# Row maxima from the high parts alone, with query tiles paired on the lower and the upper rows of the array

## The chip, the cores and the metric

The kernel runs on one core of a Trainium2 chip. Its time is in microseconds (us) of the device, and the number that counts is the median of several runs. A core has TensorE (PE in the profile; its weight loads are listed apart, as PEld), VectorE (DVE), ScalarE (ACT), GpSimd (POOL) and SyncE (SP, which here only issues DMAs). PE reads its two operands from SBUF and writes to PSUM banks; DVE and ACT read PSUM. Each engine works through its instructions in the order in which the program lists them.

## The reference, cut to what matters

One encoder layer is applied to 2048 + 256 tokens with a model width of 1024: a norm, one input projection, a bidirectional mLSTM on eight heads beside grouped-query attention on eight heads, an output projection, and a gated feed-forward block with a convolution. The attention is the part that counts here:

```
q = rmsnorm(aq per head); k = rmsnorm(ak per head); both rotated
s = q @ k^T / 8                     # per head, 64 wide, fp32
p = softmax(s, axis=-1)             # minus the row's maximum, exp, divided by the sum
o = p @ v                           # 4 query heads share one key/value head
```

The maximum that a softmax takes away leaves the result as it is, whatever number is taken away, as long as the exponentials neither overflow nor vanish.

## The kernel before, in words

Every fp32 operand of a large matmul is split into a high part in the type fp32r and the rest, its low part, and a product is the sum of high x high, high x low and low x high.

The program has five stages. Stage A projects q, k, v and the gates. Then two Python generators are run against each other by `run_both`: `attention` and `mlstm`. It counts the costs that each yields (constants such as `A_PAIR`, `A_MAX`, `A_PREP` for attention) and picks whichever is behind; a scheduler with priorities then orders the instructions on each engine, so that matmuls of the two stand mixed. When `mlstm` has ended, `attention` goes on beside `phase_c`, the output projection; there the order on PE is the order of the code. `phase_u` and `phase_e`, the feed-forward block, follow without attention.

`attention` works through 36 blocks (`hbs`), 32 of them with 2048 keys and four with 256. A block has 512 queries in four tiles of 128. For the block that comes next, `prep` loads q (`load_q`, into the tile printed as `bq`, with `QZB` = 2 buffers; it loads one block ahead), transposes it on PE into PSUM (`pq`), and ACT copies it to SBUF: `qq` holds the high part on partitions 0 to 63 and the low part on 64 to 127, and `qm` holds the high part again, with a row for the maximum. `kk` holds the high part of the keys twice, on both halves of the partitions, so that a matmul of `kk` and `qq` gives k_high x (q_high + q_low).

For the softmax a first sweep finds each query's maximum: `maxstep` does one matmul of a query tile with 512 keys (`px`, L573) and one DVE reduction over it (L574), 528 times in all. `prep2a` and `prep2b` turn the maxima into a row of `qm`. The second sweep, for the current block, is `scores` (`ps`, L599 and L600; two ACT exponentials and a DVE subtraction that give `ph` and `pl`) and `values` (`pv`, L617, six matmuls for two key tiles). `px`, `ps`, `pq` and the maxima's `pr` all take PSUM tiles of one tag, `sc`, with four buffers. In the loop over blocks, `maxstep`s of the next block are spread over the key pairs `kp` of the current one.

Of the kernel before, what the change touches and what calls it, by code (L numbers as in the profile page):

```python
# [9 lines left out]
F32 = mybir.dt.float32  # L10
F32R = mybir.dt.float32r
AF = mybir.ActivationFunctionType
ALU = mybir.AluOpType
AX = mybir.AxisListType
# [3 lines left out]
P = 128  # L18
# [6 lines left out]
HD = 64  # L25
# [29 lines left out]
APRI = 1000  # L55
WB = 8
RST = 512
QZB = 2
RWM = 4
S1B = 2  # L60
DMB = 6
# [2 lines left out]
A_PAIR = 2.3  # L64
A_MAX = 0.23
A_PREP = 1.0
# [26 lines left out]
def f32(ap):  # L93
    return ap.bitcast(F32)
# [382 lines left out]
def attention(g, tc, s1, s2, pp):  # L477


    nc = g.nc  # L480
    sp = s1
    hbs = []
# [12 lines left out]
    def load_kv(grp, k0, k1, after=None):  # L495

        if (grp, k0) in kv:
            return
        n = k1 - k0
        sp = s2 if n == NT1 else s1  # L500
        kv[(grp, k0)] = parts = []
        for t0 in range(0, n, 4):
            m = min(4, n - t0)
            s = f"{n}_{t0}"
            kk = sp.tile([P, m * P], F32R, tag="kk" + s, name=f"kk{grp}_{s}", bufs=1)
            kl1 = sp.tile([65, m * P], F32R, tag="kl1" + s, name=f"kl1{grp}_{s}", bufs=1)
            vs = [sp.tile([P, m, P if a == 0 else HD], F32R, tag=f"v{a}" + s, name=f"v{a}{grp}_{s}", bufs=1)
                  for a in range(2)]
            c = slice((k0 + t0) * P, (k0 + t0 + m) * P)
            if after is not None:  # L510
                for t in (kk[0:1, 0:1], kk[HD:HD + 1, 0:1], kl1[0:1, 0:1], vs[0][0:1, 0, 0:1], vs[1][0:1, 0, 0:1]):
                    nc.gpsimd.tensor_copy(t, after[0:1, 0:1])
            nc.gpsimd.memset(f32(vs[0][:, :, HD:]), 1.0)
            for r in (0, HD):
                nc.gpsimd.dma_start(f32(kk[r:r + HD, :]), g.k_d[grp, 0:HD, c])
            nc.gpsimd.dma_start(f32(kl1[0:HD, :]), g.k_d[grp, HD:P, c])
            nc.gpsimd.memset(f32(kl1[64:65, :]), 1.0)
            for a in range(2):
                nc.gpsimd.dma_start(f32(vs[a][:, :, 0:HD]), g.v_d[a, grp, :, k0 + t0:k0 + t0 + m])
            parts.append((kk, kl1, vs))  # L520
# [14 lines left out]
    def load_q(n):  # L535

        if n in qzs or n >= len(hbs):
            return
        t = 0
        qz = qzs[n] = sp.tile([P, 4, P], F32R, tag="qz", name=f"bq{n}", bufs=QZB)  # L540
        for h, q0, q1 in hbs[n][1]:
            nc.sync.dma_start(f32(qz[:, t:t + q1 - q0]), g.q_d[q0:q1, :, h].rearrange("n p d -> p n d"))
            t += q1 - q0

    def prep(n):

        s = HB()
        grp, s.qs, k0, k1 = hbs[n]
        load_q(n)
        load_q(n + 1)  # L550
        load_kv(grp, k0, k1)
        s.kv = kv[(grp, k0)]
        s.nq, s.nk = 4, k1 - k0
        s.N = s.nq * P
        s.nm = "%d_%d" % s.qs[0][0:2]
        qz = qzs.pop(n)
        pq = pp.tile([P, 512], F32R, tag="sc", name="pq" + s.nm)
        for t in range(s.nq):
            nc.tensor.transpose(pq[:, t * P:(t + 1) * P], qz[:, t, :], g.identr)
        s.qq = sp.tile([P, 512], F32R, tag="qq", name="qq" + s.nm, bufs=2)  # L560
        nc.scalar.activation(s.qq[:, 0:s.N], f32(pq[:, 0:s.N]), AF.Copy)
        s.qm = sp.tile([65, 512], F32R, tag="qm", name="qm" + s.nm, bufs=2)
        nc.scalar.activation(s.qm[0:HD, 0:s.N], f32(pq[0:HD, 0:s.N]), AF.Copy)
        s.mx = sp.tile([P, 4, 4], F32, tag="mx", name="mx" + s.nm, bufs=2)
        s.nsp = -(-s.nk * P // 512)
        s.todo = [(t, z) for z in range(s.nsp) for t in range(s.nq)]
        return s

    def maxstep(s):
        t, z0 = s.todo.pop(0)  # L570
        w = min(512, s.nk * P - z0 * 512)
        ps = pp.tile([P, 512], F32, tag="sc", name=f"px{s.nm}_{t}_{z0}")
        nc.tensor.matmul(ps[:, 0:w], s.qq[:, t * P:(t + 1) * P], s.kv[z0][0][:, 0:w], start=True, stop=True)  # L573
        nc.vector.tensor_reduce(s.mx[:, t, z0:z0 + 1], ps[:, 0:w], AX.X, ALU.max)  # L574

    def prep2a(s):

        nq = s.nq
        s.m4 = sp.tile([P, 4], F32, tag="m4", name="m4" + s.nm, bufs=2)
        nc.vector.tensor_reduce(s.m4[:, 0:nq], s.mx[:, 0:nq, 0:s.nsp], AX.X, ALU.max)  # L580
        s.m4r = sp.tile([P, 4], F32R, tag="m4r", name="m4r" + s.nm, bufs=2)
        nc.vector.tensor_scalar(s.m4r[:, 0:nq], s.m4[:, 0:nq], -1.0, None, ALU.mult)

    def prep2b(s):

        pr = pp.tile([P, 512], F32, tag="sc", name="pr" + s.nm)
        for t in range(s.nq):
            nc.tensor.matmul(pr[:, t * P:(t + 1) * P], s.m4r[:, t:t + 1].to_broadcast([P, P]), g.identr, start=True,
                             stop=True)
        nc.scalar.activation(s.qm[HD:HD + 1, 0:s.N], pr[HD:HD + 1, 0:s.N], AF.Copy)  # L590

    def scores(s, kp):
        N = s.N
        parts = []
        for z in range(2):
            ps = pp.tile([P, 512], F32, tag="sc", name=f"ps{s.nm}_{kp}_{z}")[:, 0:N]
            kk, kl1, _ = s.kv[kp // 2]
            kc = (2 * kp + z) % 4 * P
            nc.tensor.matmul(ps, kk[:, kc:kc + P], s.qq[:, 0:N], start=True, stop=False)  # L599
            nc.tensor.matmul(ps, kl1[:, kc:kc + P], s.qm[:, 0:N], start=False, stop=True)  # L600
            ph, pl = (sp.tile([P, 512], F32R, tag=t, name=f"{t}{s.nm}_{kp}_{z}", bufs=n)[:, 0:N]
                      for t, n in (("ph", PHB), ("pl", PLB)))
            nc.scalar.activation(ph, ps, AF.Exp)  # L603
            nc.scalar.activation(ps, ps, AF.Exp)  # L604
            nc.vector.tensor_tensor(pl, ps, f32(ph), ALU.subtract)  # L605
            parts.append((ph, pl))
        return parts
# [42 lines left out]
    def pairs(b):  # L650
        return (b[3] - b[2]) // 2

    g.a_total = sum(A_PAIR * pairs(b) + A_MAX * 4 * -(-pairs(b) // 2) + A_PREP for b in hbs)
    cur = prep(0)
    while cur.todo:
        maxstep(cur)
        yield A_MAX
# [5 lines left out]
    def value():  # L663

        s, kp, parts = todo.pop(0)
        values(s, kp, parts)
        if kp == s.nk // 2 - 1:
            while fins:
                fins.pop(0)()
            fin1(s)  # L670
            fins.extend([lambda: fin2(s)] * 4 + [lambda: fin3(s), lambda: fin4(s)])

    for n in range(len(hbs)):
        nxt = prep(n + 1) if n + 1 < len(hbs) else None
        yield A_PREP / 2
        nkp = cur.nk // 2
        ready = None
        for kp in range(nkp):
            todo.append((cur, kp, scores(cur, kp)))
            yield 0.4 * A_PAIR  # L680
            if ready:
                prep2b(ready)
                ready = None
            if nxt is not None and nxt.todo:
                if n == len(hbs) // 2 - 1:

                    k = 2 * (kp - 2) - (nxt.nq * nxt.nsp - len(nxt.todo))
                else:
                    k = -(-len(nxt.todo) // max(nkp - kp - (MXZ if g.alone else MXE), 1))
                for i in range(k):  # L690
                    maxstep(nxt)
                    if i % 2:
                        yield 2 * A_MAX
                if not nxt.todo:
                    prep2a(nxt)
                    ready = nxt
            if len(todo) > PLAG:
                value()
                yield 0.6 * A_PAIR
            for _ in range(1 if kp < nkp - 1 else 2):  # L700
                if fins:
                    fins.pop(0)()
        if nxt is not None and nxt.todo:
            while nxt.todo:
                maxstep(nxt)
            prep2a(nxt)
            ready = nxt
        if ready:
            yield A_PREP
            prep2b(ready)  # L710
        cur = nxt
# [862 lines left out]
def body(tc, aps, phases="abcd"):  # L1574
# [5 lines left out]
    with ExitStack() as st:  # L1580
# [32 lines left out]
        with ExitStack() as s2:  # L1613
# [37 lines left out]
            def after_m():  # L1651
# [4 lines left out]
                return phase_c(g, g.sn, sc, pc, (sw, swo))  # L1656

            rest = run_both(g, tc, attention(g, tc, sa, sk, pa), mlstm(g, tc, g.sm, sm2, sw, g.sn, g.pj, pm), after_m)
        s5 = st.enter_context(ExitStack())
        pd = [pool(s5, "d_u", bufs=1, space=PSUM)]  # L1660
# [116 lines left out]
```

## Time and profile before

| what | value |
|---|---|
| median of 3 runs | 3392.04 us (3388.86 to 3394.19) |
| the profiled execution | 3394.19 us, span from first to last instruction 3392.5 us |
| mean granted TensorE clock | 0.985 |
| busy: PE, PEld, DVE, ACT, POOL | 3276.5, 3049.5, 2426.0, 1779.7, 1360.6 us |
| first and last `px` matmul start | 253.2 and 1729.5 us |
| `px` matmuls (L573) | 528, 202.1 us busy, 412 ns each |
| their reductions on DVE (L574) | 528, 345.3 us busy, 670 ns each |

The time of a matmul in the profile runs from its start to its modelled end; since the next one starts while it is still passing through the array, records overlap. What a matmul costs PE is the distance from its start to the start of the next, its pitch, not its duration. So a busy PE is not yet a PE that is full; that has to be worked out from the pitches.

### The profile page before, as it was taken

How to read it: one execution, taken by the hardware profiler on the slowest of the kernel's cores; microseconds unless marked ns; L12 is line 12 of the kernel's file. 1: busy time of each engine (PE TensorE's matmuls, PEld its weight loads, DVE VectorE, ACT ScalarE, POOL GpSimd, SP SyncE). 2: the span in 40 equal slices, each digit the busy share in tenths (PEclk: the TensorE clock that was granted, in tenths of full speed). 3: DMA queues.
4: the chain of work that ended last, by engine and by line, in shares of the span. 5: the costliest groups of instructions: out<-in, count | busy, mean ns of one | idle time of the engine just before them, and what ended most of it. 6: DMA issues, size and time to landing. Idle time of an engine off the chain costs nothing. (4 is left out here: it accounts for less than half of the span.)

```text
span 3392.5 us, 57175 instructions
## 1 busy us (share of the span) xinstructions
PE 3276.5 (97%) x21402; PEld 3049.5 (90%) x21402; DVE 2426.0 (72%) x3759; ACT 1779.7 (52%) x3708; POOL 1360.6 (40%) x1684
## 2 busy tenths in 40 slices
PE   7989999999999999889999999999999999999998
PEld 6778888888888888778889999999999998999998
DVE  6875687777768878966765778878877776544464
ACT  4535666667766776655553544445555555323231
POOL 6544122213232232211245457744544442762332
PEclk9999999999999999999999999999999999999999
DMA  6766243333345444433347324425322223875463
GB/s 221 239 199 171 89 136 95 109 109 117 93 130 169 121 139 136 121 97 96 99 140 263 123 97 151 133 90 183 99 99 93 93 99 124 297 256 174 148 224 107
DMA packets 300262, 481.86 MB, mean 142 GB/s; under 512 B 36528, under 2 KB 186192, under 8 KB 299984
## 3 DMA queue, kind: packets, MB, share of 16 engines
q1 hardware_dynamic: 247600, 348.33, 32.5%
q0 software_dynamic: 35824, 120.42, 10.8%
q10 hardware_dynamic: 16560, 9.44, 0.9%
q8 instruction: 169, 2.77, 0.3%
q14 instruction: 109, 0.89, 0.1%
HBM read 336.19 MB, written 141.90 MB: 141 GB/s over the span
## 5 line engine op out<-in xcount | busy, mean ns | idle before, releaser
L605 DVE TENSOR_TENSOR pl<-ps,ph 128x512 fp32r<-128x512 f32 x520 | 352.6, 683 | 185.1 <-ACT ps L604 179.2
L1202 PE MATMUL pa<-nt,wut 128*128 128x290 f32 (+1 forms) x3168 | 448.9, 298 | 10.1 <-ACT u L1220 8.0
L1202 PEld LDWEIGHTS pa<-nt,wut 128*128 128x128 f32 x3168 | 433.1, 190 | 12.1 <-ACT u L1220 9.4
L603 ACT ACTIVATE ph<-ps 128x512 fp32r<-128x512 f32 x520 | 309.4, 595 | 252.2 <-PE ps L600 241.8
L574 DVE TENSOR_REDUCE mx<-px 128x1 f32<-128x512 f32 (+1 forms) x528 | 345.3, 670 | 76.1 <-PE px L573 74.1
L1312 DVE SCALAR_TENSOR_TENSOR y<-u,cw,y 128x1152 f32<-128x1152 f32 (+1 forms) x176 | 323.8, 1840 | 36.1 <-ACT yc L1310 17.3
L617 PE MATMUL pv<-ph,v 128*128 128x512 f32 (+1 forms) x1040 | 319.0, 400 | 0.6 <-ACT ph L603 0.3
L604 ACT ACTIVATE ps<-ps 128x512 f32<-128x512 f32 x520 | 310.3, 597 | 0.0
L1531 PE MATMUL et<-tet,wet 128*128 128x384 f32 x1584 | 281.1, 338 | 1.3 <-DVE tet L1374 0.7
L1531 PEld LDWEIGHTS et<-tet,wet 128*128 128x128 f32 x1584 | 278.7, 189 | 1.9 <-DVE tet L1374 1.1
L1045 PEld LDWEIGHTS po<-cmx,wo 128*128 128x128 f32 x1728 | 222.0, 192 | 19.3 <-ACT cmx L1032 11.4
L1045 PE MATMUL po<-cmx,wo 128*128 128x256 f32 x1728 | 226.4, 285 | 11.4 <-ACT cmx L1032 11.2
L1531 PE MATMUL e<-te,we 128*128 128x384 f32 x1188 | 212.5, 339 | 11.0 <-ACT te L1373 7.1
L1531 PEld LDWEIGHTS e<-te,we 128*128 128x128 f32 x1188 | 210.0, 190 | 12.1 <-ACT te L1373 7.3
L599 PE MATMUL ps<-qq,kk 128*128 128x512 f32 x520 | 215.5, 416 | 3.7 <-DVE mx L574 2.2
L600 PE MATMUL ps<-qm,kl 65*128 65x512 f32 x520 | 206.9, 400 | 0.0
L573 PE MATMUL px<-kk,qq 128*128 128x512 f32 (+1 forms) x528 | 202.1, 412 | 4.9 <-DVE mx L574 2.9
L763 PE MATMUL mj<-mn,wm 128*128 128x256 f32 x1296 | 202.1, 287 | 3.2 <-ACT og L777 1.9
L763 PEld LDWEIGHTS mj<-mn,wm 128*128 128x128 f32 x1296 | 185.8, 191 | 20.6 <-ACT og L777 2.0
L773 PEld LDWEIGHTS mv<-wm,mn 128*128 128x128 f32 x1296 | 184.1, 191 | 18.5 <-ACT qb L769 2.5
L773 PE MATMUL mv<-wm,mn 128*128 128x256 f32 x1296 | 197.8, 286 | 1.0 <-ACT qb L769 0.9
L617 PEld LDWEIGHTS pv<-ph,v 128*128 128x128 f32 (+1 forms) x1040 | 157.1, 163 | 37.3 <-ACT ph L603 1.8
(305 smaller groups left out, 7292.4 us busy)
## 6 DMA issues: line engine op xcount, KB each, us to landing
mn<-n_d SPq DMA_DIRECT2D x216, 256.0 KB, 3.2
ru<-w_up SPq DMA_DIRECT2D x88, 512.0 KB, 3.6
a_d<-y POOLq DMA_DIRECT2D x88, 288.0 KB, 2.6
a_d<-tc POOLq DMA_DIRECT2D x66, 288.0 KB, 3.1
n_d<-n1T SPq DMA_DIRECT2D x18, 1024.0 KB, 5.6
dm<-nm_d POOLq DMA_DIRECT2D x72, 256.0 KB, 4.0
mjn<-n_d SPq DMA_DIRECT2D x72, 256.0 KB, 3.1
mvn<-n_d SPq DMA_DIRECT2D x72, 256.0 KB, 3.2
```

The lines of the kernel that those rows point to most:

```text
L574: nc.vector.tensor_reduce(s.mx[:, t, z0:z0 + 1], ps[:, 0:w], AX.X, ALU.max)
L599: nc.tensor.matmul(ps, kk[:, kc:kc + P], s.qq[:, 0:N], start=True, stop=False)
L603: nc.scalar.activation(ph, ps, AF.Exp)
L604: nc.scalar.activation(ps, ps, AF.Exp)
L605: nc.vector.tensor_tensor(pl, ps, f32(ph), ALU.subtract)
L617: nc.tensor.matmul(s.pv[0:HD if k in (1, 3) else P, 0:N], v, p, start=(kp == 0 and k == 0), stop=(2 * kp + 2 == s.nk and k == 5))
L763: nc.tensor.matmul(pj[:, o], s.w[c][:, a, o * P:(o + 1) * P], nT[c][:, :, h, :], start=(c + o + k == 0), stop=(c == NCC - 1 and k == 2 and ...
L773: nc.tensor.matmul(pv[:, o], nT[c][:, o, a, :], s.w[c][:, h, 256:512], start=(c + o + k == 0), stop=(c == NCC - 1 and k == 2 and o == 1))
L1045: nc.tensor.matmul(po[:, o], wo[z // 2][c][:, a, n], mx[c][:, h, :], start=(c == 0 and k == 0), stop=(c == NCC - 1 and k == 2))
L1202: nc.tensor.matmul(p[:, z], w[:, aa, c, :], ops[k][:, c, bb, z * m:z * m + m], start=c == 0 and i == 0 and not add, stop=c == NCC // 2 - 1 ...
L1312: nc.vector.scalar_tensor_tensor(y[:, s:e], u[:, s + k:e + k], cw[:, k, jj:jj + 1], y[:, s:e], ALU.mult, ALU.add)
L1531: nc.tensor.matmul(ps[m // 2][:, m % 2], w[:, aa, m * P:(m + 1) * P], t[:, bb], start=p == 0 and n == 0, stop=p == NP - 1 and n == 2)
```

## The change: what it does

- `maxstep` takes two query tiles, `t` and `t + 2`, at a time, and only the high parts: a matmul of 64 rows with `qq[0:64]` and `kk[0:64]` on the lower rows of the array, then one with a new tile `qd[64:128]` and `kk[64:128]` on the upper rows. Their number and widths are the same as before (528; 512 columns, 16 of them 256), each with 64 rows in place of 128. Two PSUM tiles are taken before the first of the pair, and the two reductions follow.
- `prep` has one more ACT copy for each block, which puts the high part of query tiles 2 and 3 on partitions 64 to 127 (`qd`).
- `QZB` is 1 in place of 2, and the load of q for the block after next is moved from `prep` into the loop, at the second `kp`.
- The planner's `a_total` and the yields count a pair as one `A_MAX`.

Nothing is changed in `scores` and `values`, nor in what the reductions read.

```
-QZB = 2
+QZB = 1
...
         load_q(n)
-        load_q(n + 1)
         load_kv(grp, k0, k1)
...
         nc.scalar.activation(s.qm[0:HD, 0:s.N], f32(pq[0:HD, 0:s.N]), AF.Copy)
+        s.qd = sp.tile([P, 2, P], F32R, tag="qd", name="qd" + s.nm, bufs=1)
+        nc.scalar.activation(s.qd[HD:P], f32(pq[0:HD, s.N // 2:s.N]).rearrange("p (t n) -> p t n", t=2), AF.Copy)
...
-        s.todo = [(t, z) for z in range(s.nsp) for t in range(s.nq)]
+        s.todo = [(t, z) for z in range(s.nsp) for t in range(s.nq // 2)]
...
-        ps = pp.tile([P, 512], F32, tag="sc", name=f"px{s.nm}_{t}_{z0}")
-        nc.tensor.matmul(ps[:, 0:w], s.qq[:, t * P:(t + 1) * P], s.kv[z0][0][:, 0:w], start=True, stop=True)
-        nc.vector.tensor_reduce(s.mx[:, t, z0:z0 + 1], ps[:, 0:w], AX.X, ALU.max)
+        kk = s.kv[z0][0]
+        both = [pp.tile([P, 512], F32, tag="sc", name=f"px{s.nm}_{t + 2 * k}_{z0}")[:, 0:w] for k in range(2)]
+        nc.tensor.matmul(both[0], s.qq[0:HD, t * P:(t + 1) * P], kk[0:HD, 0:w], start=True, stop=True)
+        nc.tensor.matmul(both[1], s.qd[HD:P, t], kk[HD:P, 0:w], start=True, stop=True)
+        for k, ps in enumerate(both):
+            nc.vector.tensor_reduce(s.mx[:, t + 2 * k, z0:z0 + 1], ps, AX.X, ALU.max)
...
-    g.a_total = sum(A_PAIR * pairs(b) + A_MAX * 4 * -(-pairs(b) // 2) + A_PREP for b in hbs)
+    g.a_total = sum(A_PAIR * pairs(b) + A_MAX * 2 * -(-pairs(b) // 2) + A_PREP for b in hbs)
...
                 for i in range(k):
                     maxstep(nxt)
-                    if i % 2:
-                        yield 2 * A_MAX
+                    yield A_MAX
...
+            if kp == min(1, nkp - 1):
+                load_q(n + 2)
```

The scheduler decides where the two matmuls of a pair come to stand. On PE, in the stage with `mlstm`, one stretch of the first block with 2048 keys reads before (`mv` and `mu` are mLSTM's matmuls, `px_0_0_2` is query tile 0 with the third 512 keys):

```order
L573 MATMUL px_0_0_2_3142<-kk_16_8_2726,qq_0_2901 128x512
L617 MATMUL pv_0_3154<-pl_0_1_1_3083,v_16_0_2696 128x512
L773 MATMUL mv_4_3840<-wm_2_629,mn_4_2_3771 128x256 x2
L573 MATMUL px_0_1_2_3145<-kk_16_8_2726,qq_0_2901 128x512
L842 MATMUL mu_3_3623<-va_1_2528,kw_3_3421 128x130
L773 MATMUL mv_4_3840<-wm_3_744,mn_4_3_3772 128x256 x6
L773 MATMUL mv_4_3840<-wm_4_867,mn_4_4_3773 128x256 x5
```

and now, on PE at the same keys (L576 is the lower half of a pair, L577 the upper):

```order
L576 MATMUL px_0_0_2_3141<-kk_16_8_2725,qq_0_2905 128x512
L622 MATMUL pv_0_3153<-pl_0_1_1_3089,v_16_0_2695 128x512
L779 MATMUL mv_4_3885<-wm_4_867,mn_4_4_3818 128x256 x4
L779 MATMUL mv_4_3885<-wm_5_980,mn_4_5_3819 128x256
L577 MATMUL px_0_2_2_3142<-kk_16_8_2725,qd_0_2909 128x512
L779 MATMUL mv_4_3885<-wm_5_980,mn_4_5_3819 128x256 x5
L779 MATMUL mv_4_3885<-wm_6_1101,mn_4_6_3820 128x256
```

The pair is split by six matmuls of other work. Counted over the whole program, the 432 `px` of the stage with `mlstm` stand in 383 unbroken stretches, 341 of them one `px` long. In the stage with `phase_c`, PE before reads (`po` is the output projection)

```order
L1045 MATMUL po_0_20461<-cmx_6_20066,wo_0_18541 128x256 x3
L1045 MATMUL po_0_20461<-cmx_7_20070,wo_0_18546 128x256 x3
L573 MATMUL px_12_2_1_20503<-kk_16_4_11413,qq_12_20332 128x512
L573 MATMUL px_12_3_1_20506<-kk_16_4_11413,qq_12_20332 128x512
L617 MATMUL pv_12_20509<-ph_12_0_0_20357,v_16_0_11404 128x512
```

and now, on PE in the same stage,

```order
L1051 MATMUL po_0_20526<-cmx_6_20144,wo_0_18627 128x256 x3
L1051 MATMUL po_0_20526<-cmx_7_20148,wo_0_18632 128x256 x3
L576 MATMUL px_12_1_1_20571<-kk_16_4_11446,qq_12_20395 128x512
L577 MATMUL px_12_3_1_20572<-kk_16_4_11446,qd_12_20399 128x512
L622 MATMUL pv_12_20577<-ph_12_0_0_20405,v_16_0_11437 128x512
```

Here the pairs stay together: 96 `px` in 43 stretches, 38 of one pair and 5 of two. That makes 426 stretches in all.

On SP the loads of q move as well. At the start of attention, q of the first three blocks was loaded ahead of the eight loads of mLSTM's operand (`mn`) for its third step. Now the third block's q has moved behind them, and the second block's load waits until the first block's q has been transposed, since there is one buffer. Later the load for a block stands a few rows further down the queue than before.

More of the change, by code (lines that the diff above doesn't have):

```diff
@@ L685, in attention @@
                 if n == len(hbs) // 2 - 1:
-                    k = 2 * (kp - 2) - (nxt.nq * nxt.nsp - len(nxt.todo))
+                    k = kp - 2 - (nxt.nq // 2 * nxt.nsp - len(nxt.todo))
                 else:
```

## The prediction

> **What bounds the kernel now.** I read the stages first (busy time of each engine by stretch), then the groups inside one stretch, then single starts in the timeline. The columns of the first view are PE, PEld, DVE, ACT and POOL busy with their counts, then clock, DMA share and GB/s.
>
> ```profile
> 400.00:600.00 200.00, 200.00 (x1281) 176.44 (x1279) 158.28 (x349) 133.32 (x358) 51.03 (x106) 1.00 0.37 109
> 1500.00:1600.00 100.00, 98.94 (x626) 86.26 (x625) 70.38 (x126) 53.47 (x106) 14.70 (x16) 1.00 0.30 93
> ```
>
> The first row is attention with mLSTM, the second attention with the output projection. In both PE is hardly ever idle and DVE and ACT have a fifth to almost a half of their time free. Since matmul records overlap, I check by pitches that PE is really full. From the timeline:
>
> ```profile
> 1000.29 0.40 PE L763 MATMUL mj<-mn,wm 128*128 128x256 f32 x2
> 1000.52 0.39 PE L573 MATMUL px<-kk,qq 128*128 128x512 f32 x1
> 1000.76 0.52 PE L763 MATMUL mj<-mn,wm 128*128 128x256 f32 x3
> 1001.11 0.62 PE L617 MATMUL pv<-ph,v 128*128 128x512 f32 x2
> 1001.57 0.40 PE L599 MATMUL ps<-qq,kk 128*128 128x512 f32 x1
> ```
>
> A matmul of 256 columns has a pitch of (1000.52 - 1000.29) / 2 = 0.115 to (1001.11 - 1000.76) / 3 = 0.117 us, one of 512 columns of (1001.57 - 1001.11) / 2 = 0.23 us. In the stretch 400 to 600 the groups of PE are:
>
> ```profile
> L763 PE MATMUL mj<-mn,wm 128*128 128x256 f32 x288 | 45.9, 286 | 0.0
> L773 PE MATMUL mv<-wm,mn 128*128 128x256 f32 x288 | 45.6, 287 | 0.0
> L599 PE MATMUL ps<-qq,kk 128*128 128x512 f32 x70 | 29.0, 414 | 0.0
> L573 PE MATMUL px<-kk,qq 128*128 128x512 f32 x71 | 28.7, 417 | 0.0
> L617 PE MATMUL pv<-ph,v 128*128 128x512 f32 x70 | 28.3, 404 | 0.0
> L600 PE MATMUL ps<-qm,kl 65*128 65x512 f32 x70 | 28.2, 403 | 0.0
> L617 PE MATMUL pv<-ph,v 128*64 128x512 f32 x70 | 27.9, 399 | 0.0
> L617 PE MATMUL pv<-pl,v 128*128 128x512 f32 x68 | 25.5, 397 | 0.0
> ```
>
> 576 x 0.117 + 419 x 0.23 = 67 + 96 = 163 us. The other 286 matmuls of the 1281 have 37 us left, 0.13 each. So PE is full in this stage, and what is added to its stream or taken from it there moves the end of the stage almost one for one. `px` takes 71 x 0.23 = 16 of the 200 us, and 528 x 0.23 = 121 us in the whole program.
>
> **The change part by part.** *The 528 matmuls.* They stay 512 columns wide, so alone each still takes 0.23 us: halving the rows saves nothing by itself (`ps` with 65 rows takes as long as with 128). What can be saved is the second one of a pair, where it runs at the same time as the first, and the order in front of this text has about 93 places where a lower and an upper one stand next to each other. The bound on one side is no overlap, 0, on the other the whole pitch, 93 x 0.23 = 21 us. The trace has no two matmuls on separate rows; I take the whole 21, since a pitch of 0.23 against a record of 0.39 says that what a matmul waits for is the array's input, and these two have different inputs.
>
> The Trainium skill, in "TensorE: Matmul & The Clock Gate", Part 3, says the same of row tiles: they start about 4 ns apart and run side by side. By that it would be 93 x 0.226 = 21 us; no run so far shows it.
>
> *Going to 64 rows and back.* Before, one line alone uses at most 64 rows of the array: L428, 18 matmuls with 40 rows in three groups (the program addresses them, as it will `px`, to 64 rows; `ps` with 65 rows is addressed to all 128). The timeline around its third group, matmuls and weight loads:
>
> ```profile
> 252.46 0.28 PE L773 MATMUL mv<-wm,mn 128*128 128x256 f32 x1
> 252.67 0.57 PE L428 MATMUL gpt<-ident,rows 40*128 40x40 f32 x6
> 253.01 0.23 PE L428 MATMUL gpt<-ident,rows 40*128 40x40 f32 x1
> 253.17 0.39 PE L573 MATMUL px<-kk,qq 128*128 128x256 f32 x1
> 253.39 0.52 PE L573 MATMUL px<-kk,qq 128*128 128x256 f32 x3
> ...
> 252.67 0.45 PEld L428 LDWEIGHTS gpt<-ident,rows 40*128 40x128 f32 x6
> 253.17 0.30 PEld L573 LDWEIGHTS px<-kk,qq 128*128 128x128 f32 x2
> ...
> 1551.41 0.40 PE L600 MATMUL ps<-qm,kl 65*128 65x512 f32 x1
> 1551.19 0.19 PEld L600 LDWEIGHTS ps<-qm,kl 65*128 65x128 f32 x1
> ```
>
> Usually a weight load starts a pitch ahead of its matmul (1551.19 against 1551.41). Here it starts with it, at 252.67 and again at 253.17: nothing was loaded ahead over the border. Into L428, `mv` has a pitch of 0.21 in place of 0.12. Out of it, from the last L428 to the second `px` is 0.38, where L428's own pitch, (253.01 - 252.67) / 5 = 0.07, and one of 256 columns, 0.12, would make 0.19. So a way out costs 0.38 - 0.19 = 0.19 us: 0.09 of waiting, and a weight load in the open, which stretches the pitch of the first `px` to 0.22. A way in costs 0.09 seen directly; behind it the weights of `px` are as wide as those on the way out, so I add the same 0.10 and take 0.19. A stretch of `px` then costs 0.38, and the bound below, with both weight loads hidden, is 0.09 + 0.09 = 0.18.
>
> A stretch that narrows the columns costs nothing, as these rows of the timeline show:
>
> ```profile
> 277.02 0.36 PE L773 MATMUL mv<-wm,mn 128*128 128x256 f32 x1
> 277.23 0.62 PE L617 MATMUL pv<-ph,v 128*128 128x512 f32 x2
> 277.69 0.52 PE L773 MATMUL mv<-wm,mn 128*128 128x256 f32 x3
> ```
>
> The second of these two `pv` has 64 columns of weights, and both together take 0.46, 0.23 each. "TensorEngine Tiling (Array Packing)" of the Trainium skill, Key Properties, says that changing the tiling mode drains TensorE. The trace agrees with it for rows (L428) and not for columns (`pv`). By that rule the sum is the one below; by what `pv` shows it would be the first rival.
>
> Stretches: 383 beside mLSTM and 43 beside the output projection, 426. Cost 426 x 0.38 = 162 us; with 0.18 it is 77 us.
>
> *The reductions, the extra copy, the loads of q.*
>
> ```profile
> L574 DVE TENSOR_REDUCE mx<-px 128x1 f32<-128x512 f32 (+1 forms) x528 | 345.3, 670 | 76.1 <-PE px L573 74.1
> L563 ACT ACTIVATE qm<-pq x36: 575/580/611, 248.5 to 1693.6; 64x512 fp32r<-64x512 f32 x36
> L542 SPq DMA_DIRECT2D bq<-q_d x56: 359/371/990, 240.3 to 1601.5; - x56
> DMA to landing us min/median/max: 2.1/2.8/6.0
> ```
>
> The reductions are the same 528; two come at once, but DVE waited 74 us for `px` before, so it has the room. The copy `qd`, half as wide as `qm`'s 0.58 us, comes 36 times: between 36 x 0.29 = 10 and 36 x 0.58 = 21 us of ACT, which has a third of its time free; I cost it at nothing, and if a first `px` pair of each block had to wait for it, at those 21 us. One buffer for q: in a block with 2048 keys the load has the block's remaining `kp`s, tens of us, against 2.8; only at the four blocks with 256 keys can a landing show, 4 x 2.8 = 11 us. Nobody waited for `bq` in the trace. Behind such a load on SP stand `mn` loads, whose buffers run a whole step ahead. I cost it at nothing. The planner's counts fall for `px` alone, in the total and in the steps alike, so attention keeps its share of the interleaving.
>
> **Sum.** 162 - 21 = +141 us on the profiled execution's 3394.2, that is 3535; the median shown is 2.2 lower, so 3533. Nothing takes this up: `phase_u` and `phase_e` start when attention and the output projection have ended.
>
> **The rivals.**
> 1. *Faster: the border is free for rows as it is for `pv`'s columns.* Then the overlap alone is left, -21 us, 3371. It decides from a stretch that costs under 21 / 426 = 0.05 us. For it speaks `pv`; against it that all the borders of L428 that the timeline shows are late. The group before:
>
> ```profile
> 247.42 0.54 PE L559 MATMUL pq<-identr,bq 128*128 128x128 f32 x4
> ...
> 247.70 0.25 PE L559 MATMUL pq<-identr,bq 128*128 128x128 f32 x1
> 247.88 0.25 PE L428 MATMUL gpt<-ident,rows 40*128 40x40 f32 x1
> ```
>
> The last `pq` of four and the first L428 behind it: 0.18 from a matmul whose pitch inside its own group is (247.70 - 247.42) / 3 = 0.09. But L428 had few neighbours, and its lateness could be its own.
> 2. *The border costs only the waiting, 0.18.* 77 - 21 = +56, 3448. For it: `px` on one half of the rows might let the other half's weights load ahead. Against: the load at 253.17.
> 3. *The pairs don't overlap*, so the change does not do what it says even where they stand together: +162, 3554. The trace has nothing on either side.
> 4. *Waits for `sc` on top.* A pair takes two of four buffers at once, and PE would wait for a reduction, 0.67 us, at the pairs that stand together: up to 81 x 0.67 = 54 more, 3587.
>
> **How the numbers follow.** Forecast 3533: 0.51. Rival 2: 0.17. Rival 3: 0.16. Rival 4 and the exposed copies and loads: 0.05. Rival 1: 0.09, of which 0.02 so near to zero that it could not be told. A further 0.02 is for no difference by a mix of these. The range from 3440 to 3575 leaves out rival 1, the mix, the lower part of rival 2 (0.04) and rival 4: 0.20. A measurement of this kernel can tell about 0.2%, 7 us, from nothing. Faster 0.07, same 0.04, slower 0.89.
>
> **What the profile would show.** If I am right, the pitch into a lone `px` is 0.09 longer than the matmul ahead of it needs, its weight load starts with it and not a pitch ahead, and so does that of the matmul behind it; two `px` of a pair side by side start within hundredths of a microsecond; the last `px` starts some 140 us later, around 1870 where it was 1729.5; the reductions keep their 0.67 us and DVE's busy share in 400 to 600 falls. I am wrong if lone `px` matmuls keep the pitch of 0.23 and their weight loads are ahead, or if PE's idle time before `px` or `ps` grows to tens of us.

## The result, and the profile after

The changed kernel takes 3546.1 us in the median of four runs, against 3393.1 us of the kernel before on the same chip: a ratio of 1.045, with a 95% interval of 1.043 to 1.047. The forecast was 3533 us: the change costs 153 us where 141 were worked out. The profiled execution has a span of 3546.5 us.

The stages of the kernel after, in the same view by stretch (PE, PEld, DVE, ACT, POOL busy with counts, clock, DMA):

```profile
400.00:600.00 200.00, 200.00 (x1149) 159.02 (x1148) 140.67 (x298) 119.53 (x313) 43.97 (x88) 1.00 0.33 98
1650.00:1750.00 100.00, 98.72 (x583) 80.59 (x583) 63.90 (x114) 48.58 (x96) 13.42 (x14) 0.97 0.25 77
```

PE is as busy as before and gets less done: 1149 matmuls in 200 us, where there were 1281. DVE, ACT and the weight loads all fall. PE's busy share alone would have shown nothing of this.

The groups of PE in that stretch have the reason in the mean duration (last but one column, ns) of one line:

```profile
L604 PE MATMUL ps<-qq,kk 128*128 128x512 f32 x61 | 25.2, 413 | 0.0
L605 PE MATMUL ps<-qm,kl 65*128 65x512 f32 x61 | 24.3, 399 | 0.0
L577 PE MATMUL px<-kk,qd 64*128 64x512 f32 x32 | 15.9, 497 | 0.0
L576 PE MATMUL px<-kk,qq 64*128 64x512 f32 x31 | 15.4, 497 | 0.0
```

`px` had a mean of 417 ns on 128 rows and has 497 on 64. The timeline of the kernel after shows a lone `px` among mLSTM's matmuls and the weight loads beside it:

```profile
709.94 0.40 PE L779 MATMUL mv<-wm,mn 128*128 128x256 f32 x2
710.27 0.50 PE L576 MATMUL px<-kk,qq 64*128 64x512 f32 x1
710.70 0.51 PE L622 MATMUL pv<-pl,v 128*128 128x512 f32 x1
711.04 0.40 PE L779 MATMUL mv<-wm,mn 128*128 128x256 f32 x2
...
710.27 0.18 PEld L576 LDWEIGHTS px<-kk,qq 64*128 64x128 f32 x1
710.70 0.19 PEld L622 LDWEIGHTS pv<-pl,v 128*128 128x128 f32 x1 [0.24 <-issue]
710.80 0.43 PEld L779 LDWEIGHTS mv<-wm,mn 128*128 128x128 f32 x2
```

The first two `mv` take 0.33 us to the start of `px` where two pitches make 0.23 to 0.24: 0.09 of waiting on the way in. `px` has a pitch of 0.43 where 0.23 is usual, that is its own weight load in the open and the waiting on the way out. `pv` behind it has 0.34 for 0.23: its weight load, which starts with it at 710.70 and not a pitch ahead. Together 0.09 + 0.20 + 0.11 = 0.40. Over the 266 lone `px` with neighbours of 512 or 256 columns, the median is 0.39 (0.62 beyond what the neighbours take, against 0.23 before).

A pair that stands together, beside the output projection:

```profile
1719.17 1.58 PE L1051 MATMUL po<-cmx,wo 128*128 128x256 f32 x12
1720.68 0.50 PE L576 MATMUL px<-kk,qq 64*128 64x512 f32 x1
1720.68 0.49 PE L577 MATMUL px<-kk,qd 64*128 64x512 f32 x1
1721.10 1.20 PE L622 MATMUL pv<-ph,v 128*128 128x512 f32 x4
```

Both start at 1720.68; the second costs nothing. In the whole trace 76 of the 101 places where a lower and an upper `px` follow each other are like this, with starts 3 or 4 ns apart; at the others the second one comes later. But the two borders cost as much as around a lone one, and a pair together, in the median of 53, takes 0.63 us beyond its neighbours where two `px` before took 0.47. So even where the pairing works, it loses 0.16 us.

### The profile page after: what moved, and what is told of

It reads as the page before. It is cut to its first block, busy times and chain, and to the rows that moved or that the text cites. A ratio compares the mean times of both kernels' runs of the same rounds, so it can differ in the third digit from the quotient of the medians.

```text
span 3546.5 us, 57252 instructions
## 1 busy us (share of the span) xinstructions
PE 3430.9 (97%) x21402; PEld 3052.5 (86%) x21402; DVE 2433.3 (69%) x3759; ACT 1798.0 (51%) x3744; POOL 1367.6 (39%) x1684
## 5 line engine op out<-in xcount | busy, mean ns | idle before, releaser
L622 PE MATMUL pv<-ph,v 128*128 128x512 f32 (+1 forms) x1040 | 328.4, 412 | 0.0
L622 PE MATMUL pv<-pl,v 128*128 128x512 f32 x520 | 202.9, 421 | 0.0
```

The lines of the kernel that those rows point to most:

```text
L622: nc.tensor.matmul(s.pv[0:HD if k in (1, 3) else P, 0:N], v, p, start=(kp == 0 and k == 0), stop=(2 * kp + 2 == s.nk and k == 5))
```

## The experiments

The theory is that going from matmuls on the whole array to matmuls on 64 rows and back costs about 0.39 us for each unbroken stretch of `px`, and that little else of the change matters. The rivals are the rest of the change (the loads of q, the copy, the PSUM tiles taken two at a time), the smaller number of rows by itself, and pairs that do not overlap.

**Everything but the rows.** The changed kernel with `px` on 128 rows:

```
-        nc.tensor.matmul(both[0], s.qq[0:HD, t * P:(t + 1) * P], kk[0:HD, 0:w], start=True, stop=True)
-        nc.tensor.matmul(both[1], s.qd[HD:P, t], kk[HD:P, 0:w], start=True, stop=True)
+        nc.tensor.matmul(both[0], s.qq[:, t * P:(t + 1) * P], kk[:, 0:w], start=True, stop=True)
+        nc.tensor.matmul(both[1], s.qq[:, (t + 2) * P:(t + 3) * P], kk[:, 0:w], start=True, stop=True)
```

> The changed kernel with all its other parts (pairs of query tiles, two PSUM tiles taken at once, the extra ACT copy, one buffer for q, the moved loads, the planner's counts), but each px matmul on all 128 rows again, as before the change; the copy on the upper partitions is made and not read. If the border between 64 and 128 rows is what costs (0.39 us for a stretch of px in the changed kernel's trace), the 153 us go: 3385 to 3400 us. If the loads, the copy or the PSUM tiles taken in pairs cost, the time stays above 3420; if they are all of it, at 3546.

Measured: 3405.3 us, 1.0038 (1.0026 to 1.0051) times before. The rows are 141 of the 153 us, and the rest of the change is 12 to 13, a little more than I had allowed.

**The rows alone, 64 and 65 of them.** The kernel before, with one line changed, `n` being 64 or 65:

```
-        nc.tensor.matmul(ps[:, 0:w], s.qq[:, t * P:(t + 1) * P], s.kv[z0][0][:, 0:w], start=True, stop=True)
+        nc.tensor.matmul(ps[:, 0:w], s.qq[0:n, t * P:(t + 1) * P], s.kv[z0][0][0:n, 0:w], start=True, stop=True)
```

> The kernel before, with one edit: px uses rows 0 to 63 alone (the high parts), nothing is paired. Its px stand in 433 unbroken stretches on PE. Border theory: 433 x 0.39 = 169 us more than before, nothing overlaps, 3562 us (3540 to 3575). If the change's time comes from its pairing, loads or copy, it stays at 3393.

> The same one edit to the kernel before, with 65 rows (the high parts and one row of the low part), which are addressed to the whole array. Border theory: no border, so 3393 us, within 0.3%. If it is the smaller number of rows itself, or weights loaded into a part of the rows, it is as slow as with 64 rows, 3560.

Measured: with 64 rows 3548.8 us, 1.0464 (1.0448 to 1.0480); with 65 rows 3395.4 us, 1.0012 (1.0003 to 1.0021). One row decides over 153 us. The lines of `px` in the two traces (duration ns min/median/max, then first and last start):

```profile
L573 PEld LDWEIGHTS px<-kk,qq x528: 182/183/330, 250.4 to 1875.1; 64*128 64x128 f32 x176
L573 PE MATMUL px<-kk,qq x528: 276/493/793, 250.5 to 1875.3; 64*128 64x512 f32 x170, 64*128 64x256 f32 x6
```

```profile
L573 PEld LDWEIGHTS px<-kk,qq x528: 186/189/330, 251.2 to 1728.8; 65*128 65x128 f32 x176
L573 PE MATMUL px<-kk,qq x528: 276/397/792, 251.2 to 1729.0; 65*128 65x512 f32 x170, 65*128 65x256 f32 x6
```

The first is of 64 rows, the second of 65. The median duration grows by 0.10 us, as much as the weight load in the open, and the last `px` comes 146 us later. Over 433 stretches the 157 us are 0.36 each, somewhat less than the 0.39 of the timeline.

That it is the stretch that pays, and not each `px`, is seen where two `px` stand together in the run with 64 rows:

```profile
1719.86 0.39 PE L600 MATMUL ps<-qm,kl 65*128 65x512 f32 x1
1720.18 0.73 PE L573 MATMUL px<-kk,qq 64*128 64x512 f32 x2
1720.84 1.33 PE L1045 MATMUL po<-cmx,wo 128*128 128x256 f32 x9
```

`ps` has a pitch of 0.32, 0.09 more than usual, and the two `px` take 0.66 where two pitches make 0.46: 0.20 more, as for the lone one above. Over the 43 stretches of two `px` and the 8 of three with neighbours of 512 or 256 columns, the median is 0.40 us above their pitches, about the same as the 0.39 of one.

**Half of the `px`.** As the last one, but only the first two groups of 512 keys use 64 rows:

```
+        n = HD if z0 < 2 else P
```

> The kernel before with px on 64 rows for the first two groups of 512 keys alone (272 of 528), on 128 rows for the others. The px with 64 rows stand in some 216 stretches. Border theory: 216 x 0.39 = 84 us more than before, 3476 us, about half of what lower_64 took. A cost paid once, or one that sets in with the stage as a whole, would give 3392 or 3549.

Measured: 3470.0 us, 1.0238 (1.0219 to 1.0256), 77 us more than before for 216 stretches: 0.36 each again. So the cost is paid each time and not once. This run by itself can't tell stretches from single `px`, since both are about halved (272 of 528 `px`, 0.28 us each, against 0.30 with all of them); the stretches of two and three above can.

**Pairs on the same rows.** The changed kernel, but the second of a pair uses the lower rows too:

```
-        nc.tensor.matmul(both[1], s.qd[HD:P, t], kk[HD:P, 0:w], start=True, stop=True)
+        nc.tensor.matmul(both[1], s.qq[0:HD, (t + 2) * P:(t + 3) * P], kk[0:HD, 0:w], start=True, stop=True)
```

> The changed kernel with one edit: the second px of a pair uses the lower rows too (qq in place of qd), so that two px next to each other cannot run at the same time; borders and stretches (426) stay as they are. If the overlap is real, 102 places x 0.23 us are given back: 3546 + 23 = 3569 us (3562 to 3576). If pairs gain nothing, 3546.

Measured: 3560.7 us, 1.0500 (1.0486 to 1.0515) times before, where the changed kernel has 1.045 (1.043 to 1.047). Each against its own runs of before, that is 169 and 153 us, so some 16 us of overlap are lost, of the 23 expected; the two intervals do not overlap. The 23 counted each of the 102 places in the order on PE (101 in the order of the starts); the 76 at which two `px` really start together make 76 x 0.23 = 17. Its timeline shows such a pair:

```profile
1713.41 0.49 PE L576 MATMUL px<-kk,qq 64*128 64x512 f32 x1
1713.75 0.39 PE L577 MATMUL px<-kk,qq 64*128 64x512 f32 x1
1714.07 1.19 PE L622 MATMUL pv<-ph,v 128*128 128x512 f32 x4
```

0.66 us from the first start to `pv`, 0.42 in the changed kernel (1720.68 to 1721.10): 0.24 of overlap at such a place.

**Pairs kept together, first try.** The two matmuls in a critical section of the scheduler:

```
+        with tc.tile_critical():
             nc.tensor.matmul(both[0], ...)
             nc.tensor.matmul(both[1], ...)
```

> The changed kernel with the two matmuls of a pair in one critical section for the scheduler, so that they stand together: 250 stretches in place of 426, 278 places where the next px is on the other half of the rows in place of 102. Border theory with overlap: 176 stretches fewer x 0.39 and 176 more overlaps x 0.23 save 109 us, 3437 us; without overlap 3478. Rival, waits for two free PSUM tiles at once: little is saved, 3520 or more, and PE's waits for DVE before px grow.

Measured: 3924.8 us, 1.157 (1.155 to 1.158). The stretches became 250, and the time rose by some 380 us over the changed kernel, far from what any theory said. The stage and the longest waits that name `px`:

```profile
600.00:800.00 200.00, 168.70 (x961) 136.56 (x959) 111.75 (x246) 101.84 (x285) 44.54 (x92) 0.93 0.25 75
...
PEld px L577 <- issue: 397.2, 264, 7.9
...
PE px L577 <- DMA og_d<-og: 17.2, 6, 3.7
```

PE is idle for 31 of 200 us, the weight loads of the sections' first matmuls have 397 us of idle time ahead of them (264 times, once for each), and `px` is held by things that it does not use, such as a DMA of mLSTM's gate. The section itself waits, so this run says nothing on the border; it only says that a critical section is no way to keep two matmuls together here.

**Pairs kept together, second try.** The pair's PSUM as one tile of two banks, with two `sc` tiles in place of four; and the same with `px` on 128 rows:

```
-SCB = 4
+SCB = 2
...
-        both = [pp.tile([P, 512], F32, tag="sc", name=f"px{s.nm}_{t + 2 * k}_{z0}")[:, 0:w] for k in range(2)]
+        two = pp.tile([P, 2, 512], F32, tag="px", name=f"px{s.nm}_{t}_{z0}", bufs=1)
+        both = [two[:, k, 0:w] for k in range(2)]
```

> The changed kernel with the pair's two PSUM banks as one tile of its own (and two sc tiles in place of four), so that the scheduler can put a pair together: 283 stretches, 245 places where lower and upper stand next to each other. It is to be compared with onetile_full, which has the same PSUM tiles. Border theory: 283 x 0.39 - 245 x 0.23 = 54 us above onetile_full. If a border cost less than the overlap gains, it would be below it; if lone and paired px cost alike, 110 us above.

> The same PSUM tiles as in onetile, with px on all 128 rows as before the change: what two sc tiles in place of four cost by themselves. If PE's waits for sc are small, 3400 to 3430 us; if four tiles were needed, up to 528 x 0.23 = 120 us more, 3510. No border here by any theory.

Measured: 3628.9 us, 1.0698 (1.0682 to 1.0715), with 64 rows and 3580.2 us, 1.0553 (1.0538 to 1.0569), with 128. The difference is 49 us, 54 were expected: with the pairs mostly together (245 overlaps, 283 stretches), 64 rows still lose. That this use of PSUM costs 189 us by itself was a miss; I had allowed 120 at most. It is two things at once, two `sc` tiles in place of four and a single tile for the pairs of `px`, and no run separates them. PE's waits in the run with 128 rows name DVE:

```profile
PE px L577 <- DVE mx L580: 33.6, 32, 4.2
PE ps L605 <- DVE pl L611: 27.2, 28, 2.6
```

These are a part of it. The stages also meet in another way: mLSTM's last `mT` starts at 1275.6 us (before: 1444.9) and the output projection at 1613.4 (before: 1456.5), so that attention stands alone on PE for 338 us, where it had been 12. In that stretch the run with 128 rows has

```profile
1276.00:1613.00 337.00, 268.04 (x901) 168.58 (x900) 223.22 (x361) 185.74 (x353) 23.85 (x30) 0.84 0.10 29
```

PE is idle for 69 of the 337 us, at a granted clock of 0.84. How the 189 us divide is not shown. Nor is PE full there, as the 54 us assumed, so these two runs support the border less sharply than 64 rows against 65.

**The remaining 12 us.** Three edits tell the rest of the change apart: the loads alone on the kernel before; the run with 128 rows without the copy `qd`; and that one with the planner's counts as before.

```
-QZB = 2
+QZB = 1
...
-        load_q(n + 1)
...
+            if kp == min(1, nkp - 1):
+                load_q(n + 2)
```

> The kernel before with one part of the change alone: one buffer for q and the moved loads. full_rows left 13 us that are not the border. If they come from the loads, 3405 us; if from taking PSUM tiles in pairs or from the extra copy, 3392, as before.

```
-        s.qd = sp.tile([P, 2, P], F32R, tag="qd", name="qd" + s.nm, bufs=1)
-        nc.scalar.activation(s.qd[HD:P], f32(pq[0:HD, s.N // 2:s.N]).rearrange("p (t n) -> p t n", t=2), AF.Copy)
```

> full_rows without the extra ACT copy: px on all 128 rows, two at a time, with the moved loads and the planner's counts. full_rows was 13 us above before, and the loads alone are nothing. If the 13 us come from taking PSUM tiles in pairs, 3405 us; if from the copy, 3392.

```
-    g.a_total = sum(A_PAIR * pairs(b) + A_MAX * 2 * -(-pairs(b) // 2) + A_PREP for b in hbs)
+    g.a_total = sum(A_PAIR * pairs(b) + A_MAX * 4 * -(-pairs(b) // 2) + A_PREP for b in hbs)
...
-                    yield A_MAX
+                    yield 2 * A_MAX
```

> pairs_only with the planner's counts as before the change (a pair counts as two A_MAX). pairs_only was 12 us above before. If taking PSUM tiles in pairs is what costs, 3405 us again; if the counts that move attention against mLSTM and the output projection, 3393.

Measured: the loads alone 3391.6 us, 1.0003 (0.9995 to 1.0012), nothing. Without the copy 3405.3 us, 1.0038 (1.0024 to 1.0053); with the old counts besides, 3403.9 us, 1.0035 (1.0021 to 1.0048). So neither copy nor counts nor loads. By exclusion it is in working two query tiles at a time: in the other order, or in the two PSUM tiles taken at once, which no run tells apart. The output projection of before, of the run with 128 rows, and of that run without the copy, first and last start:

```profile
L1045 PE MATMUL po<-cmx,wo x1728: 274/282/581, 1456.5 to 1851.0; 128*128 128x256 f32 x192
```

```profile
L1051 PE MATMUL po<-cmx,wo x1728: 274/282/580, 1455.5 to 1858.5; 128*128 128x256 f32 x192
```

```profile
L1049 PE MATMUL po<-cmx,wo x1728: 274/282/580, 1456.3 to 1853.1; 128*128 128x256 f32 x192
```

In the second it starts a microsecond earlier and lasts 403.0 us in place of 394.5, which would put 8 of the 12 us into this stage. But in the third, with the same time over its runs, it lasts 396.8. So where the 12 us arise, and in which wait, is not shown.

## Why the prediction was right, point by point

- *PE is full, so what is added moves the end.* Right: the last `px` came at 1871.0 us where it had been 1729.5, and around 1870 was said.
- *0.38 us for a stretch.* Right: 0.39 by the timeline, 0.09 of waiting and 0.10 of weight load on the way in, and the same again on the way out. The way into 64 rows with a weight load as wide as that of `px` was the one part that the trace of before did not show; it is 0.10, as taken from the way out. By the times of whole runs a stretch is 0.36; where the difference goes is not shown.
- *The bound below, 0.18, with hidden weight loads (rival 2).* Refuted: the load starts with its matmul on both sides, at 710.27 and at 710.70.
- *The border is free (rival 1).* Refuted by 64 rows against 65. That changing the tiling mode drains TensorE, in "TensorEngine Tiling (Array Packing)" of the Trainium skill, Key Properties, agrees with what the runs show for rows (0.39 us a stretch); for 64 columns, `pv` keeps its pitch of 0.23 us.
- *The overlap, 21 us, taken whole without a row to stand on (rival 3 said 0).* Right in kind, and the size was partly luck: a place where both start together gives 0.24 us, but there are 76 of them and not 93, and in whole runs the overlap is some 16 us. The Trainium skill's start of row tiles about 4 ns apart ("TensorE: Matmul & The Clock Gate", Part 3) agrees with the 3 or 4 ns at these 76 places.
- *Copy, loads and planner at nothing.* Right, each by its own run. The copy took 0.38 us each (0.29 to 0.58 was said), and `px` waited for it for some 2 us in all.
- *The reductions two at a time at nothing (rival 4: up to 54 us).* Mis-sized, if it is they: working two tiles at a time costs 12 us, about as much as lies between 3533 and 3546; rival 4's waits are at most a part of them, since PE's idle time before `px` that ends with a reduction is 2.9 us before, 5.1 in the changed kernel, and 7.9 and 3.1 in the runs with 128 rows with and without the copy.
- *The sum.* The rows cost 141 us, which is what 162 - 21 gave. By whole runs both terms were too large: they would be 426 x 0.36 = 153 and 16, which makes 137. So the closeness of the sum is partly luck.
- *DVE falls in 400 to 600.* Right: 158.3 to 140.7 us. The reductions kept their duration (674 ns for 670).

## What to carry to other kernels

Matmuls on half of the rows run side by side, but by the numbers here only an unbroken stretch of several would pay for its two borders: a stretch costs 0.39 us here, and each overlap gives 0.23 back, so that one pair loses, and two pairs in a row would about break even. The few stretches of two pairs in the changed kernel do not show a gain, since the second pair waits for its PSUM tiles there:

```profile
1837.01 0.50 PE L577 MATMUL px<-kk,qd 64*128 64x512 f32 x1
1838.05 0.50 PE L576 MATMUL px<-kk,qq 64*128 64x512 f32 x1 [0.54 <-DVE pl L610]
```

Where a scheduler mixes two streams of matmuls, count the stretches in the order that it makes, not the pairs in the source, and keep everything that is mixed on the whole array; 65 rows cost 0.1% where 64 cost 4.6%. To see such a cost in a profile, look at whether each weight load starts a pitch ahead of its matmul or together with it.

## What the runs showed of the hardware that I had not expected

The bill for the border is twofold and the same in both directions: 0.09 us of waiting, and 0.10 us of a weight load that starts with its matmul and not a pitch ahead. 64 rows against 65 is the whole difference (3548.8 and 3395.4 us), while `pv` with 64 columns of weights has the same pitch of 0.23 us as with 128. I had also not expected how much the PSUM tiles weigh in this program: with `px` in a tile of two banks and two `sc` tiles in place of four, the kernel on full rows takes 3580 us, 5.5% more, and attention then stands alone on PE for 338 us.
